# A two-layer encoder kernel on one core: the mixer's front in another order, and 1/rms spread over rows by two products

## The chip, the core and the metric

The kernel runs on one NeuronCore of one Trainium2 chip, as one launch. The metric is the device time of that launch in microseconds. Engines are named as in the profile: PE is TensorE (PEld its weight loads), DVE is VectorE, ACT is ScalarE, POOL is GpSimd, SP is SyncE, which here only issues DMA transfers.

## What is computed

Two sequences, one of 512 rows (s) and one of 1024 rows (p), each 1024 wide in float32, go through the same two layers. The reference, cut:

```python
def rms_norm(x, g):
    return x * rsqrt(mean(x * x, axis=-1, keepdims=True) + 1e-6) * g

def fourier_mixer(x, g, w):                     # layer 0
    h = rms_norm(x, g).reshape(b, s, 8, 128)
    return real(fft2(h, axes=(1, 3), norm="ortho")).reshape(b, s, d) @ w

def attention_mixer(x, ...):                    # layer 1: 8 heads, 2 kv heads, QK norm, rotary
    ...
def swiglu_ffn(x, g, w_gate, w_up, w_down):     # after each mixer, inner width 2816
    h = rms_norm(x, g)
    return (silu(h @ w_gate) * (h @ w_up)) @ w_down

for i in range(2):
    x = x + mixer_i(x)
    x = x + swiglu_ffn(x, ...)
```

## The kernel before, in words

**Precision.** Large products are made of float32 numbers split into a high part (cast to fp32r) and the rest (fp32r as well): `split` makes the high part on ACT and the rest on DVE or POOL, and `mm3` (lines 245 to 249) adds three products, high by high, high by rest, rest by high. Weights are split when they are loaded: `weights` (lines 266 to 279) issues the DMA on SP, casts on ACT (L278) and subtracts on POOL (L279). A few small products use float32 operands directly: a product with `ones` sums columns (L299) or spreads a value (L308).

**Blocks and stages.** The rows lie in three blocks of 512 columns (b = 0 for s, 1 and 2 for p). `weave` runs a main stage, the feed-forward product `ffn` of one block, together with an auxiliary stage for the next blocks, and draws from both generators in proportion to costs in the code. Ahead of this stands the front, in which only s has work: `lead` and `follow` (lines 1172 to 1195). The order on each engine is then made by a scheduler from the order in which the instructions are recorded and from its own estimate of when their operands are there; instructions that go through `pinned` keep their recorded order.

**The front.** The mixer of s has these steps.
1. `load_rows` brings the rows of s in four tiles. `in_rows(gx...)` spreads the gains over all partitions (two calls). `busy(36)` issues 36 float32 products of `ones` with itself.
2. `prepared` (lines 386 to 402): for each of four row tiles a square with a sum on ACT (L393), then four additions or products on DVE (L396 to L399) that fold the rows; then `rsqrt` (lines 282 to 293), twelve steps of 4 columns on DVE (three Newton steps), which gives `r_s`, 1/rms per row.
3. `unit(k, c)`: scales and adds the folded rows (L466 on ACT, L467 on DVE) and splits the result (`comb`). Four units; each needs `r_s`.
4. `along` multiplies the units with the Fourier matrix (`c<-mat_s,comb`); the result is split into `u` (tile `eo`).
5. Beside this `turned_weights` (lines 601 to 655) takes the mixer's weights `wf` through the inner Fourier transform: eight pieces. `operand(n)` adds on DVE (L619) and subtracts on POOL (L620) the two halves of a loaded piece into `f`, casts `f` on ACT (L622) and subtracts on POOL (L623) into `wm`; `product(n)` multiplies (`g<-wm,eo`), splits (`w`), and copies the two results to be written to `cwd` in DRAM, from where p reads them later. The first of the two copies runs on ACT (L644), the second on DVE (L646). The rows for column 64 come as one stacked piece, `raw<-in_wf64`, into `stage`, which `stacked` casts on ACT (L597) and subtracts on DVE (L599).
6. `mixer_projection` multiplies `u` with the turned weights, eight steps n (`c<-eo,w`), adds to the residual, splits, and squares. Then `in_rows(rstd[0])`, and the first feed-forward product `g<-h,w` starts.

**What sets the order between 3 and 5.** `lead` draws one step of `turned_weights` after the steps 1, 3, 6, 8, 10, 12, 14 of the mixer, and records `stacked` after step 4. `follow` draws one more after each of the first four projection steps, and then the rest.

**Spreading.** `in_rows(y)` (lines 302 to 309) is used throughout: for gains, for 1/rms of a block ahead of each `normed` or `moving`, for the keys. For each of four chunks of 128 columns ACT scales the identity by a column of y (L307), and a product with `ones` in float32 (L308) puts that column's values into every partition:

```python
for j in range(4):
    dg = (temp or tmp)(P)
    act.activation(dg, ident, AF.Copy, scale=y[:, j : j + 1])
    pe.matmul(r[:, j * P : (j + 1) * P], ones, dg, start=True, stop=True)
```

Of the kernel before, what the change touches and what calls it, by code (L numbers as in the profile page):

```python
# [10 lines left out]
F32 = mybir.dt.float32  # L11
# [6 lines left out]
P = 128  # L18
# [106 lines left out]
def trunk_kernel(ctx: ExitStack, tc: tile.TileContext, t: dict):  # L125
# [89 lines left out]
    make_identity(nc, ident)  # L215
    ones = cp.tile([P, P], F32, name="ones")
    dve.memset(ones, 1.0)
# [63 lines left out]

    def rsqrt(y, x, scale, scr):

        n = y.shape[-1]
        v, ti, a = (scr[:, k * n : (k + 1) * n] for k in range(3))
        z = col(n)
        dve.tensor_scalar(v, x, scale, EPS, op0=ALU.mult, op1=ALU.add)
        dve.tensor_scalar(ti.bitcast(I32), v.bitcast(I32), 1, None, op0=ALU.logical_shift_right)
        dve.tensor_scalar(z.bitcast(I32), ti.bitcast(I32), -1.0, MAGIC, op0=ALU.mult, op1=ALU.add)
        for k in range(3):  # L290
            dve.tensor_tensor(a, v, z, op=ALU.mult)
            dve.scalar_tensor_tensor(a, a, -0.5, z, op0=ALU.mult, op1=ALU.mult)
            dve.scalar_tensor_tensor(z if k < 2 else y, a, 1.5, z, op0=ALU.add, op1=ALU.mult)

# [7 lines left out]
    def in_rows(y, temp=None, ps=None):  # L302

        r = bank() if ps is None else ps
        for j in range(4):
            dg = (temp or tmp)(P)
            act.activation(dg, ident, AF.Copy, scale=y[:, j : j + 1])  # L307
            pe.matmul(r[:, j * P : (j + 1) * P], ones, dg, start=True, stop=True)  # L308
        return r
# [76 lines left out]
    def prepared(seq, n, ga, gb, sums):  # L386


        s = mpt.tile([P, n], F32, name=f"s_{seq}")
        r = mpt.tile([P, n], F32, name=f"r_{seq}")  # L390
        for c, x in enumerate(whole[seq]):
            sq = raw_tile(D) if seq == "p" else bank2().rearrange("p k n -> p (k n)")
            pinned(act.activation(sq, x, AF.Square, accum_out=s[:, c : c + 1]))  # L393
            y = tl("c", [TB], F32, "cX", pools["psX"])
            f = sums[c]
            dve.tensor_tensor(f[:, 0], ga, x[:, 0:TB], op=ALU.mult)  # L396
            dve.tensor_tensor(y, gb, x[:, TB:D], op=ALU.mult)
            dve.tensor_tensor(f[:, 1], f[:, 0], y, op=ALU.subtract)
            dve.tensor_tensor(f[:, 0], y, f[:, 0], op=ALU.add)  # L399
            yield 4.0  # L400
        rsqrt(r, s, 1.0 / D, bank()[:, 0 : 4 * n])
        return r
# [198 lines left out]
    def turned_weights(w64, dd, odd, alt):  # L601
# [26 lines left out]
        def product(n):  # L628
# [5 lines left out]
            for k in range(2):  # L634
# [7 lines left out]
                c = tl("t", [TB], F32, "tX")  # L642
                if k == 0:
                    act.copy(c, ps)  # L644
                else:
                    dve.tensor_copy(c, ps)  # L646
                sp.dma_start(cwd[h][:, :, k, j, :], c.rearrange("p (n c) -> p n c", n=4))
# [144 lines left out]
    def moving(blocks, gain, ops):  # L792

        tp = open_pool("tT")
        yield 2.0
        r = [in_rows(rstd[b], lambda n: tl("t", [n], F32, "tT", tp)) for b in blocks]
        yield 1.0
# [361 lines left out]
    xrs_s = [slot[:, 6288 + TB * i : 6288 + TB * (i + 1)] for i in range(2)]  # L1159
    stage = tl("raw", [D], F32, "rawF")  # L1160
    slot_a = h_slot("wm", F32R, "B")[:, 0 : 16 * TB].rearrange("p (s h k n) -> p s h k n", s=4, h=2, k=2)
# [10 lines left out]
    def lead():  # L1172
# [3 lines left out]
        for k, v in enumerate(m):  # L1176
            yield v
            if k == 4:
                stacked(w64[0:96], stage[0:96], 64)
            if k in (1, 3, 6) or k in (8, 10, 12, 14):  # L1180
                next(ws)

    def follow():
        m = mixer_projection("s", got_s)
        for k in range(4):
            next(m)
# [176 lines left out]
```

## Time and profile before

| | us |
|---|---|
| median of 3 runs | 3044.05 |
| lowest, highest | 3040.32, 3046.63 |
| the profiled execution | 3041.73 |
| its span, first to last instruction | 3040.0 |
| PE busy in it | 2967.5 |

The profile shows one execution. In a row of a timeline stand the start, the duration, the engine, the line, the operation, and result and operands by the program's names; in brackets how long the engine had been idle before and which instruction ended that. Matmul durations overlap: a 128x512 product shows 0.39 us and starts 0.23 us behind the one before it, so that work on PE is measured from start to start. The granted clock of PE is a share of 2.4 GHz.

### The profile page before, as it was taken

To read this page: it belongs to the slowest core of one execution; us is meant where nothing else is said; L and a number is where in the kernel's file an instruction comes from. 1 tells how busy PE (TensorE), PEld (TensorE's weight loads), DVE (VectorE), ACT (ScalarE), POOL (GpSimd) and SP (SyncE) were. 2 spreads that over 40 slices of the span, in tenths; PEclk is the share of its full clock that TensorE was granted. 3 is DMA by queue.
4 is the path that set the end of the run, shared out by engine and by line. 5 is a ranking of instruction groups with operands and counts; after the bars stand their busy time and mean duration, and the time that the engine had idled before them with its cause. 6 is when DMAs were issued, how large, how long until landed. Compare 5 with 4: busy or idle time off the path is not lost. (4 is left out here: it accounts for less than half of the span.)

```text
span 3040.0 us, 36889 instructions
## 1 busy us (share of the span) xinstructions
PE 2967.5 (98%) x14184; PEld 2435.7 (80%) x14184; DVE 1667.8 (55%) x2883; ACT 1231.3 (41%) x1835; POOL 1282.6 (42%) x652
## 2 busy tenths in 40 slices
PE   7999999999999999999999999999999999999999
PEld 6778888888877788888878788877787787887777
DVE  7785565634556543533474465665236555655566
ACT  5533332423466522333344577776324222222221
POOL 4334444433333644444433311313636644645452
PEclk9999999999999999999999999999999999999999
DMA  6434543332232633433343211212635411111111
GB/s 223 150 111 132 166 139 104 125 104 77 97 98 90 229 131 133 141 106 101 99 142 111 87 59 53 75 51 91 221 121 183 164 56 54 44 56 55 44 55 63
DMA packets 132080, 330.05 MB, mean 109 GB/s; under 512 B 14176, under 2 KB 28512, under 8 KB 131264
## 3 DMA queue, kind: packets, MB, share of 16 engines
q1 hardware_dynamic: 130688, 318.71, 32.3%
q0 software_dynamic: 928, 7.94, 0.7%
q8 instruction: 111, 1.82, 0.3%
q10 hardware_dynamic: 288, 1.05, 0.1%
q14 instruction: 65, 0.53, 0.1%
HBM read 280.45 MB, written 47.19 MB: 108 GB/s over the span
## 5 line engine op out<-in xcount | busy, mean ns | idle before, releaser
L279 POOL TENSOR_TENSOR w<-raw,w 128x1024 fp32r<-128x1024 f32 x354 | 847.2, 2404 | 1308.1 <-ACT w L278 1259.2
L745 DVE TENSOR_TENSOR acc<-c,acc 128x512 f32<-128x512 f32 x704 | 483.0, 689 | 441.4 <-PE c L249 437.3
L278 ACT CAST w<-raw 128x1024 fp32r<-128x1024 f32 x354 | 371.2, 1050 | 562.3 <-PE c L249 270.9
L247 PE MATMUL g<-h,w 128*128 128x512 f32 x1408 | 556.5, 395 | 4.4 <-ACT t L777 4.4
L249 PE MATMUL g<-h,w 128*128 128x512 f32 x1408 | 552.8, 393 | 0.8 <-POOL w L279 0.8
L248 PE MATMUL g<-h,w 128*128 128x512 f32 x1408 | 552.3, 393 | 0.0
L247 PE MATMUL c<-mid,w 128*128 128x512 f32 x1056 | 417.6, 397 | 13.0 <-DVE acc L745 8.8
L248 PE MATMUL c<-mid,w 128*128 128x512 f32 x1056 | 414.2, 392 | 1.8 <-DVE mid L241 1.8
L249 PE MATMUL c<-mid,w 128*128 128x512 f32 x1056 | 413.6, 392 | 0.0
L241 POOL TENSOR_TENSOR w<-raw,w 128x512 fp32r<-128x512 f32 (+1 forms) x178 | 239.6, 1368 | 311.0 <-ACT w L240 290.0
L858 DVE TENSOR_TENSOR acc<-c,acc 128x512 f32<-128x512 f32 x352 | 240.8, 689 | 186.4 <-PE c L249 185.5
L247 PEld LDWEIGHTS g<-h,w 128*128 128x128 f32 x1408 | 265.6, 189 | 57.5 <-ACT t L777 5.4
L249 PEld LDWEIGHTS g<-h,w 128*128 128x128 f32 x1408 | 265.6, 189 | 56.5 <-POOL w L279 1.8
L248 PEld LDWEIGHTS g<-h,w 128*128 128x128 f32 x1408 | 265.7, 189 | 52.0
L247 PEld LDWEIGHTS c<-mid,w 128*128 128x128 f32 x1056 | 198.1, 188 | 75.1 <-DVE acc L745 18.5
L248 PEld LDWEIGHTS c<-mid,w 128*128 128x128 f32 x1056 | 198.9, 188 | 42.0 <-DVE mid L241 3.8
L249 PEld LDWEIGHTS c<-mid,w 128*128 128x128 f32 x1056 | 198.6, 188 | 40.4
L248 PE MATMUL c<-h,w 128*128 128x512 f32 x480 | 188.2, 392 | 3.1 <-POOL h L241 2.9
L247 PE MATMUL c<-h,w 128*128 128x512 f32 x480 | 189.1, 395 | 0.0
L240 ACT CAST w<-raw 128x512 fp32r<-128x512 f32 (+1 forms) x178 | 107.5, 648 | 196.9 <-PE a L249 79.8
L249 PE MATMUL c<-h,w 128*128 128x512 f32 x480 | 187.0, 390 | 0.0
L1073 DVE TENSOR_REDUCE col<-a 128x1 f32<-128x1024 f32 (+1 forms) x96 | 100.4, 1046 | 127.4 <-PE a L249 127.1
(342 smaller groups left out, 4765.5 us busy)
## 6 DMA issues: line engine op xcount, KB each, us to landing
raw<-in_down_dram SPq DMA_DIRECT2D x110, 512.0 KB, 3.5
raw<-in_gate_dram SPq DMA_DIRECT2D x88, 512.0 KB, 3.5
raw<-in_up_dram SPq DMA_DIRECT2D x88, 512.0 KB, 3.6
raw<-in_qkv_dram SPq DMA_DIRECT2D x36, 512.0 KB, 3.9
t<-xres SPq DMA_DIRECT2D x56, 256.0 KB, 3.9
raw<-in_wo_dram SPq DMA_DIRECT2D x24, 512.0 KB, 3.7
raw<-in_gate_dram SPq DMA_DIRECT2D x44, 256.0 KB, 2.6
raw<-in_up_dram SPq DMA_DIRECT2D x44, 256.0 KB, 3.1
```

Of the source, the lines that this page charges most:

```text
L240: act.copy(hi, src)
L241: eng.tensor_tensor(lo, src, hi.bitcast(F32), op=ALU.subtract)
L247: pe.matmul(out, lh, rh, start=first, stop=False)
L248: pe.matmul(out, lh, rl, start=False, stop=False)
L249: pe.matmul(out, ll, rh, start=False, stop=last)
L278: pinned(act.copy(flat[:, 0], raw)) if early else act.copy(flat[:, 0], raw)
L279: pool.tensor_tensor(flat[:, 1], raw, flat[:, 0].bitcast(F32), op=ALU.subtract)
L745: dve.tensor_tensor(acc[dc], ps, acc[dc], op=ALU.add)
L858: dve.tensor_tensor(acc, ps, acc, op=ALU.add)
L1073: dve.tensor_reduce(st[:, 0:1], s_in, op=ALU.max, axis=AX.X)
```

## The change

- `prepared`: for s the four squares are recorded first, one behind the other, the steps of `rsqrt` are pinned, and the mixer yields after every second row tile rather than after each.
- `lead`: a step of `turned_weights` after the steps 0, 1, 2, 4, 6, 8, 10, 12 of the mixer (after 1, 3, 6, 8, 10, 12, 14 before); `stacked` after step 3; `follow` draws one more after three projection steps.
- `stage` takes a buffer of the tag "mid" and not one of the two of "rawF", which `f` uses.
- `product`: both copies for `cwd` run on ACT.
- `in_rows`: the four scaled identities are written side by side, each split into a high part (ACT) and the rest (DVE), and two products of 128x512 with fp32r operands take the place of four of 128x128 in float32. `ones` is made as fp32r and seen as float32 where it was used so.

```diff
-    ones = cp.tile([P, P], F32, name="ones")
+    ones_r = cp.tile([P, P], F32R, name="ones")
+    ones = ones_r.bitcast(F32)
...
-    def rsqrt(y, x, scale, scr):
+    def rsqrt(y, x, scale, scr, keep=lambda ins: ins):
...
         for k in range(3):
-            dve.tensor_tensor(a, v, z, op=ALU.mult)
+            keep(dve.tensor_tensor(a, v, z, op=ALU.mult))
...
     def in_rows(y, temp=None, ps=None):
 
         r = bank() if ps is None else ps
+        dg = [(temp or tmp)(TB, F32R) for _ in range(2)]
         for j in range(4):
-            dg = (temp or tmp)(P)
-            act.activation(dg, ident, AF.Copy, scale=y[:, j : j + 1])
-            pe.matmul(r[:, j * P : (j + 1) * P], ones, dg, start=True, stop=True)
+            js = slice(j * P, (j + 1) * P)
+            split(dg[0][:, js], dg[1][:, js], ident, gain=y[:, j : j + 1])
+        for b in range(2):
+            pe.matmul(r, ones_r, dg[b], start=b == 0, stop=b == 1)
         return r
...
-        for c, x in enumerate(whole[seq]):
+        def square(c, x):
             sq = raw_tile(D) if seq == "p" else bank2().rearrange("p k n -> p (k n)")
             pinned(act.activation(sq, x, AF.Square, accum_out=s[:, c : c + 1]))
+
+        if seq == "s":
+            for c, x in enumerate(whole[seq]):
+                square(c, x)
+        for c, x in enumerate(whole[seq]):
+            if seq == "p":
+                square(c, x)
...
-            yield 4.0
-        rsqrt(r, s, 1.0 / D, bank()[:, 0 : 4 * n])
+            if seq == "p" or c % 2:
+                yield 4.0
+        rsqrt(r, s, 1.0 / D, bank()[:, 0 : 4 * n], *([pinned] if seq == "s" else []))
...
                 c = tl("t", [TB], F32, "tX")
-                if k == 0:
-                    act.copy(c, ps)
-                else:
-                    dve.tensor_copy(c, ps)
+                act.copy(c, ps)
...
-    stage = tl("raw", [D], F32, "rawF")
+    stage = tl("stage", [D], F32, "mid")
...
-            if k == 4:
+            if k == 3:
                 stacked(w64[0:96], stage[0:96], 64)
-            if k in (1, 3, 6) or k in (8, 10, 12, 14):
+            if k < 3 or k % 2 == 0 and k < 14:
                 next(ws)
...
-        for k in range(4):
+        for k in range(3):
             next(m)
             next(ws)
```

DVE, at the end of Newton's steps of s, before the change. `r_s` is 1/rms, `eo` from `raw` the residue of the stacked weights, `f` the addition of a weight piece, `comb` a unit's split result, `w` from `g` a split turned product:

```order
L599 TENSOR_TENSOR eo_150<-raw_152,eo_150 32x1024
L291 TENSOR_TENSOR c_274<-c_274,col_275 128x4
L292 SCALAR_TENSOR_TENSOR c_274<-c_274,col_275 128x4
L293 SCALAR_TENSOR_TENSOR r_s<-c_274,col_275 128x4
L407 TENSOR_TENSOR m_290<-r_s,mask 128x1
L437 TENSOR_SCALAR neg_s<-r_s 128x4
L508 TENSOR_SCALAR t_295<-x_229,r_s 1x512
L408 TENSOR_SCALAR m_290<-m_290 128x1
L241 TENSOR_TENSOR w_328<-g_329,w_328 128x512
L467 SCALAR_TENSOR_TENSOR a_299<-x_229,m_290,a_299 128x512
```

The same place on DVE now:

```order
L292 TENSOR_TENSOR c_274<-c_274,col_275 128x4
L293 SCALAR_TENSOR_TENSOR c_274<-c_274,col_275 128x4
L294 SCALAR_TENSOR_TENSOR r_s<-c_274,col_275 128x4
L630 TENSOR_TENSOR f_288<-raw_255 128x512
L418 TENSOR_TENSOR m_295<-r_s,mask 128x1
L448 TENSOR_SCALAR neg_s<-r_s 128x4
L519 TENSOR_SCALAR t_300<-x_229,r_s 1x512
L419 TENSOR_SCALAR m_295<-m_295 128x1
L478 SCALAR_TENSOR_TENSOR a_304<-x_229,m_295,a_304 128x512
L630 TENSOR_TENSOR f_338<-raw_272 128x512
L242 TENSOR_TENSOR eo_150<-t_300,eo_150 1x512
L242 TENSOR_TENSOR comb_222<-a_304,comb_222 128x512
```

The residue of the stacked weights has left Newton's steps (it stands now behind the first `comb`), and the additions of the third and the fourth weight piece, which stood behind both first units, stand among them.

PE, where the queries' stage of the second block begins, spreading its 1/rms (`c` from `t` and `ones`) among feed-forward products (`g`, `c` from `mid`) and the first products of a projection (`c` from `h`), before the change:

```order
L247 MATMUL c_13807<-mid_13727,w_13351 128x512
L248 MATMUL c_13807<-mid_13727,w_13351 128x512
L249 MATMUL c_13807<-mid_13727,w_13351 128x512
L308 MATMUL c_13140<-t_13141,ones 128x128
L308 MATMUL c_13140<-t_13144,ones 128x128
L308 MATMUL c_13140<-t_13147,ones 128x128
L247 MATMUL c_13176<-h_12514,w_13173 128x512
L308 MATMUL c_13140<-t_13150,ones 128x128
L248 MATMUL c_13176<-h_12514,w_13173 128x512
```

The same place now:

```order
L249 MATMUL g_13745<-h_12199,w_13732 128x512
L311 MATMUL c_13140<-t_13141,ones 128x512
L248 MATMUL c_13176<-h_12514,w_13173 128x512
L311 MATMUL c_13140<-t_13142,ones 128x512
L249 MATMUL c_13176<-h_12514,w_13173 128x512
L250 MATMUL c_13176<-h_12514,w_13173 128x512
```

Four products of 128 columns have become two of 512, with one other product between them.

## Rows read from the trace of the kernel before

**Rows 1.** The page's first part: busy time, share of the span and instructions of each engine.

```profile
PE 2967.5 (98%) x14184; PEld 2435.7 (80%) x14184; DVE 1667.8 (55%) x2883; ACT 1231.3 (41%) x1835; POOL 1282.6 (42%) x652
```

**Rows 2.** Busy time by stretch of the span: stretch in us, its length, busy us of PE, PEld, DVE, ACT and POOL with their instructions, granted clock of PE, share of the DMA engines, GB/s.

```profile
0.00:5.11 5.11, 0.00 (x0) 0.00 (x1) 0.17 (x1) 1.94 (x4) 2.94 (x10) 1.00 0.61 179
...
20.01:57.45 37.44, 26.78 (x110) 19.17 (x109) 32.02 (x59) 22.30 (x43) 22.24 (x14) 0.82 0.65 205
57.45:91.84 34.39, 32.51 (x236) 30.07 (x235) 29.21 (x64) 18.36 (x33) 8.60 (x7) 1.00 0.44 129
91.84:130.00 38.16, 34.87 (x161) 28.54 (x160) 20.93 (x42) 18.75 (x31) 18.00 (x8) 0.96 0.59 207
```

**Rows 3.** PE's waits in the first 130 us: for whom, us in total, times, longest.

```profile
PE c L308 <- ACT t L307: 5.1, 1, 5.1
PE g L247 <- ACT t L644: 4.0, 2, 3.4
PE g L247 <- ACT t L777: 2.5, 1, 2.5
...
```

**Rows 4.** PE's waits from 130 us to the end, the same columns.

```profile
PE a L247 <- ACT p L1077: 12.5, 9, 1.7
...
PE c L308 <- ACT t L307: 1.3, 2, 0.9
...
```

**Rows 5.** DVE in order of time: folding steps, the first of Newton's steps, and so on to the last write into u.

```profile
12.33 1.29 DVE L397 TENSOR_TENSOR c<-c,x 128x512 f32<-128x512 f32 x2
13.53 1.28 DVE L398 TENSOR_TENSOR x<-x,c 128x512 f32<-128x512 f32 x2
...
20.39 0.15 DVE L287 TENSOR_SCALAR c<-s_s 128x4 f32<-128x4 f32 x1
...
24.97 2.54 DVE L599 TENSOR_TENSOR eo<-raw,eo 32x1024 fp32r<-32x1024 f32 x1
...
27.95 0.16 DVE L293 SCALAR_TENSOR_TENSOR r_s<-c,col 128x4 f32<-128x4 f32 x1
...
57.00 0.76 DVE L241 TENSOR_TENSOR eo<-c,eo 128x256 fp32r<-128x256 f32 x2
```

**Rows 6.** DVE's groups of instructions from 20 to 60 us: line, operation, result and operands, shapes, count, busy us, mean ns of one, idle time before them.

```profile
L619 DVE TENSOR_TENSOR f<-raw 128x512 f32<-128x512 f32 x6 | 6.4, 1076 | 1.3 <-DMA raw<-in_wf_dram 1.3
L646 DVE COPY t<-g 128x512 f32<-128x512 f32 x5 | 3.4, 677 | 0.0
...
L467 DVE SCALAR_TENSOR_TENSOR a<-x,r_s,a 128x512 f32<-128x512 f32 x1 | 0.7, 749 | 0.0
...
L496 DVE SCALAR_TENSOR_TENSOR t<-x,r_s,col 128x24 f32<-128x24 f32 x1 | 0.2, 246 | 0.0
```

**Rows 7.** ACT's groups of instructions from 20 to 60 us, columns as in rows 6.

```profile
L644 ACT COPY t<-g 128x512 f32<-128x512 f32 x5 | 2.9, 589 | 0.2
```

**Rows 8.** POOL in order of time, the weight pieces of the front.

```profile
15.06 1.27 POOL L620 TENSOR_TENSOR f<-raw 128x512 f32<-128x512 f32 x1 [11.17 <-DMA raw<-in_wf_dram]
...
24.07 2.35 POOL L623 TENSOR_TENSOR wm<-f,wm 128x1024 fp32r<-128x1024 f32 x1 [2.24 <-ACT wm L622]
26.51 3.35 POOL L620 TENSOR_TENSOR f<-raw 128x512 f32<-128x512 f32 x2
39.69 4.70 POOL L623 TENSOR_TENSOR wm<-f,wm 128x1024 fp32r<-128x1024 f32 x2 [9.83 <-ACT wm L622]
...
63.76 2.40 POOL L623 TENSOR_TENSOR wm<-f,wm 128x1024 fp32r<-128x1024 f32 x1 [1.77 <-ACT wm L622]
```

**Rows 9.** PE in order of time: the projection's first product and the first product of the feed-forward stage.

```profile
57.45 0.39 PE L247 MATMUL c<-eo,w 128*128 128x258 f32 x1
...
91.84 0.39 PE L247 MATMUL g<-h,w 128*128 128x512 f32 x1
```

**Rows 10.** Stretches of 2 us, columns as in rows 2.

```profile
40.00:42.00 2.00, 2.00 (x6) 1.18 (x5) 0.94 (x2) 1.58 (x4) 2.00 (x1) 0.50 0.95 257
50.00:52.00 2.00, 2.00 (x16) 1.85 (x16) 2.00 (x2) 0.92 (x3) 1.92 (x2) 1.00 1.18 341
```

**Rows 11.** Line 308's products over the whole span: count, durations in ns (min/median/max), first and last start.

```profile
L308 PE MATMUL c<-t,ones x136: 270/275/582, 5.1 to 2274.2; 128*128 128x128 f32 x136
...
L308 PE MATMUL a<-t,ones x16: 272/275/349, 105.9 to 115.0; 128*128 128x128 f32 x16
```

**Rows 12.** PE in order of time around the spread for a key.

```profile
738.73 0.39 PE L247 MATMUL g<-h,w 128*128 128x512 f32 x1
738.96 0.64 PE L308 MATMUL c<-t,ones 128*128 128x128 f32 x4
739.36 0.48 PE L247 MATMUL c<-h,w 128*128 128x512 f32 x1
739.68 0.65 PE L308 MATMUL c<-t,ones 128*128 128x128 f32 x4
740.08 0.48 PE L248 MATMUL c<-h,w 128*128 128x512 f32 x1
740.39 0.39 PE L249 MATMUL c<-h,w 128*128 128x512 f32 x1
```

**Rows 13.** Line 307 on ACT: four diagonals in a row in order of time, and one of them over the whole span (ns, min/median/max).

```profile
558.48 1.28 ACT L307 ACTIVATE t<-ident,rs 128x128 f32<-128x128 f32 x4 [4.96 <-DVE rs L293]
...
L307 ACT ACTIVATE t<-ident,rs x36: 384/391/404, 101.7 to 2273.3; 128x128 f32<-128x128 f32 x36
```

More of the change, by code (lines that the diff above doesn't have):

```diff
@@ L286, in rsqrt @@
         z = col(n)
-        dve.tensor_scalar(v, x, scale, EPS, op0=ALU.mult, op1=ALU.add)
-        dve.tensor_scalar(ti.bitcast(I32), v.bitcast(I32), 1, None, op0=ALU.logical_shift_right)
-        dve.tensor_scalar(z.bitcast(I32), ti.bitcast(I32), -1.0, MAGIC, op0=ALU.mult, op1=ALU.add)
+        keep(dve.tensor_scalar(v, x, scale, EPS, op0=ALU.mult, op1=ALU.add))
+        keep(dve.tensor_scalar(ti.bitcast(I32), v.bitcast(I32), 1, None, op0=ALU.logical_shift_right))
+        keep(dve.tensor_scalar(z.bitcast(I32), ti.bitcast(I32), -1.0, MAGIC, op0=ALU.mult, op1=ALU.add))
         for k in range(3):
-            dve.tensor_tensor(a, v, z, op=ALU.mult)
-            dve.scalar_tensor_tensor(a, a, -0.5, z, op0=ALU.mult, op1=ALU.mult)
-            dve.scalar_tensor_tensor(z if k < 2 else y, a, 1.5, z, op0=ALU.add, op1=ALU.mult)
+            keep(dve.tensor_tensor(a, v, z, op=ALU.mult))
+            keep(dve.scalar_tensor_tensor(a, a, -0.5, z, op0=ALU.mult, op1=ALU.mult))
+            keep(dve.scalar_tensor_tensor(z if k < 2 else y, a, 1.5, z, op0=ALU.add, op1=ALU.mult))
     def rstd_cols(y, sq, n):
@@ L795, in moving @@
         yield 2.0
-        r = [in_rows(rstd[b], lambda n: tl("t", [n], F32, "tT", tp)) for b in blocks]
+        r = [in_rows(rstd[b], lambda n, dt: tl("t", [n], dt, "tT", tp)) for b in blocks]
         yield 1.0
```

## The prediction

> **What bounds the kernel now.** I read the page's busy times first: TensorE (PE) is busy for 2967.5 of 3040.0 us, 98%, and no other engine reaches 56% [rows 1]. So only two things can move the time: work that leaves PE, and PE's idle 72.5 us. Second I read the stretches. Of the idle time 21 us lie before 130 us [rows 2]: 5.1 us before the first product, 10.7 us in the stretch from 20.01 to 57.45 us (26.78 busy of 37.44), 1.9 us up to 91.84 us, 3.3 us up to 130 us. The other 51 us are spread over 2910 us. In the stretch 20.01 to 57.45 PE also ran at a mean granted clock of 0.82: at 40 us it stands at 0.50, that is at 1.2 GHz, with gaps in PE's work ahead, and at 50 us it is back at 1.00 [rows 10]. Third come PE's waits. Before 130 us PE waits once for the first diagonals (5.1 us), then above all for copies and an activation of ScalarE (ACT) [rows 3]; after 130 us the largest wait is for attention's exponentials, which the change doesn't touch [rows 4].
>
> Fourth, the front's own chain on VectorE (DVE). It starts Newton's steps at 20.39 us and writes r_s at 27.95 us [rows 5]. Twelve small steps of about 0.2 us are 2.4 us; between them stand a split of a product, an addition and above all the residue of the stacked weights, 2.54 us [rows 5]. Everything of the mixer stands behind r_s. From 20.39 to the last write into u at 57.74 us (57.00 + 0.74) DVE is 37.35 us on its way. The projection's first product starts at 57.45 us and the first gate product at 91.84 us [rows 9]; between the two PE is busy 32.51 of 34.39 us [rows 2].
>
> **The change, part by part.**
>
> *Spreading by two products.* A spread was four fp32 products of 128 columns, two records each, so eight records. There are 152 records [rows 11], so 19 spreads; two stand ahead of the first real work, 17 behind it. What one costs PE is read at 738.96 us: up to 740.39 us there are eight records and two 128x512 products [rows 12]. 1.43 us less two products of 0.23 us (738.73 to 738.96) is 0.97 us. Now it is two products of 128x512 with fp32r operands, of the kind whose pace is 0.23 us: 0.46 us. 17 x (0.97 - 0.46) = **8.7 us less on PE**, which is the bound in all these stages. Bounds: 0, if the new products ran no faster than the old, and 9.
>
> *What the two products wait for.* Before, the first product went as soon as one diagonal was there; four take ACT 1.28 us [rows 13]. Now the first needs all four high parts, some 0.9 us more (1.28 less the 0.39 of one [rows 13]), and the second the last of four new subtractions on DVE. No row shows those at 128x128; between 128x24 (0.246 us) and 128x512 (0.749 us) [rows 6] a straight line gives 0.35 us. 17 x 4 x 0.35 = 24 us of DVE work, hidden beside PE, since DVE is busy 55% [rows 1]; without that cover the normalized operands come later. Both orders put other products between and ahead of the two, so I take 0.2 us of standing per spread, **3.4 us more**; bounds 0 and 0.9 x 17 = 15 us. The value lies near the low end because before the change PE waited for diagonals only twice behind 130 us, 1.3 us together [rows 4]. The Trainium skill (SBUF — State Buffer, "SBUF: two separate sides") says that a DVE instruction with two SBUF inputs and a GpSimd instruction take a shared pair of ports in turn, and whichever starts first holds it to its end. By that rule each subtraction could stand behind a whole POOL instruction, and the sum would be that of the last rival below. The trace agrees where it shows the case: the residue of the stacked weights began inside a POOL piece and ended 1.1 us behind that piece's end [rows 5, 8].
>
> *Front, up to r_s.* The squares now stand in a row on ACT, Newton's steps in a row on DVE, and the stacked weights' residue behind them. Taken away between 20.39 and 27.95 us: the 2.54 us [rows 5]. The order behind VectorE's start also puts the two units of x_140 together, but then an addition waits for the first weights, which POOL also got only at 15.06 us [rows 8], so that nothing is won there. r_s comes at about 25.6 us, 2.5 us earlier; bounds 0 and 3.
>
> *Front, r_s to the last u.* DVE loses the four copies that stand in this stretch (0.68 us each [rows 6], 2.7 us) and gets the residue back. Adding up its new order with 0.6 us for a 128x512 step (four take the 2.4 us from 12.33 to 14.7 [rows 5]), 1.8 for the residue (half-way between its 2.54 us and the 1.1 us that it took once POOL was done) and 1.0 for an addition that meets POOL [rows 6] gives 25.6 us, against 29.6 before (28.11 to 57.74); beside the copies the difference is standing, 1.3 us of it ahead of the additions [rows 6]. ACT gets those copies as well, 0.59 us each [rows 7], and its own list behind r_s also sums to 26 us: it becomes as full as DVE. So neither can end before 51.5 us, and some waits on PE and POOL will stay; I take 54 us, **3.5 us earlier**. The weight pieces don't hold it: POOL stood still from 29.86 to 39.69 us, waiting for a cast [rows 8], and now the additions stand among the units and a second buffer of that tag is free. Its last piece, ended at 66.16 us, should be done by 57.
>
> *Front, projection.* One more of the eight turned products stands ahead of the projection than before, 9 products of 0.23 us, so 2.1 us less remain in a stretch that PE fills; the half clock ahead of it costs what it did. **2 us earlier.** Together the first gate product moves by 5.5 us; bounds 0 and 8.6 (57.74 - 51.2, plus 2.1).
>
> *The first 20 us.* The first spread ends a good microsecond earlier, but behind it the warming products only end earlier too, and PE's next products need the first weight piece, whose halves POOL began to subtract at 15.06 us, when they had landed [rows 8]: nothing.
>
> *SP, POOL.* SP issues as many transfers; the loads of wf are moved ahead of the writes of cwd, whose reader is far off. Nothing.
>
> Sum: -8.7 + 3.4 - 5.5 = -10.8. The profiled execution took 3041.73 us (span 3040.0), so 3030.9, and I forecast **3031 us**. The median of the runs shown, 3044.05, is 2.3 us above the profiled execution; I leave that in the range.
>
> **The rivals.** A measurement of this kernel can tell 0.2%, 6.1 us, from no change.
>
> *Spreads stand still (same or a little faster).* Each of the four subtractions reads two operands in SBUF, as the additions f do, and those took 1.08 us on average [rows 6] where POOL was at work, and the residue 2.54 us: it began at 24.97 us, POOL's piece ended at 26.42 us, and the residue at 27.51 us [rows 5, 8]. POOL is busy 42% [rows 1] with pieces of 2.4 us [rows 8]; a subtraction that meets one waits 1.2 us for its rest, 0.5 us on average, and 17 of them take 8.6 us off, all that the products give. Then the front alone is left: 3041.7 - 5.5 = 3036.
>
> *Front gives nothing.* ACT takes DVE's place there: its eight copies stand in one queue with the casts that PE waits for, and each copy also waits for a buffer that a write to cwd must free. Then only the spreads are left: -8.7 + 3.4, 3036.4.
>
> *The new products bring nothing.* If `ones` as fp32r with these operands went at the old pace of 0.97 us per spread and the front's lead were lost at the first gate units, where PE already waits 2.5 us for the activation [rows 3], it stays at 3041.
>
> *Slower.* The same standing, but worse: the four subtractions of a spread meet POOL's pieces not once but so that a spread comes 1.2 us late each time, with PE queued behind its first product in order and every product behind it. 17 x 1.2 = 20.4, less 8.7 and 5.5: 3041.7 + 6.2 = 3048. It decides from 0.84 us per spread on ((8.7 + 5.5) / 17). For it: no row shows the subtractions, and the additions f beside POOL took on average as much as this asks. Against it: POOL idles more than half of the time, and a spread lost its 1.2 us only if the scheduler left no slack. The Trainium skill's rule on the shared ports, named above, would make this case.
>
> **How the numbers follow.** Both gains as summed: 0.58. Spreads stand still: 0.15. Front gives nothing: 0.14. Nothing comes: 0.05. Slower: 0.08. The first lies nearly whole beyond -6.1 us from the median (0.56 of it), the second and third straddle the bound (0.17 of 0.29): faster 0.73, slower 0.08, same 0.19. Range: from 3022, where the front's 8.6 and the spreads' 9 come with hardly a wait and the execution is like the profiled one, to 3043, which takes in all cases but the slower one.
>
> **What would show it.** Right: two records of 128x512 per spread at a pace of about 0.23 us; r_s written near 25.6 us; the last write into u near 54 us; the first gate product near 86 us; POOL's last piece of wf before 60 us; PE busy some 10 us shorter with about the same idle time. Wrong: waits of PE for L245 or L244 at the spreads of 0.5 us and more each; subtractions at 128x128 of over 1 us beside POOL; u late behind ACT's copies; or idle time of PE grown by as much as its busy time shrank.

## The result: slower, and the profile after

The changed kernel takes 3049.02 us (median of 12 runs, 3043.97 to 3053.47), the kernel before 3042.68 beside it (3038.26 to 3046.63): a ratio of 1.0024 [1.0017, 1.0032]. The forecast was 3031 us. In the profiled execution the span grew by 7.5 us, from 3040.0 to 3047.5. The page's first part of the changed kernel, to be held against [rows 1]:

```profile
PE 2965.1 (97%) x14070; PEld 2430.7 (80%) x14070; DVE 1702.6 (56%) x2951; ACT 1235.3 (41%) x1843; POOL 1283.6 (42%) x652
```

PE's busy time fell by 2.4 us, not by some 10, and its idle time rose by 9.9 us to 82.4. The products themselves did nearly what was forecast. From 404.95 to 1524.91 us before and from 404.10 to 1518.69 us after, PE runs the same products but for those of nine spreads (columns as in [rows 2]). Its work there shrank by 4.42 us, 0.49 per spread, and the stretch by 5.37 us: so far the spreads paid. First before, then the change:

```profile
404.95:1524.91 1119.96, 1110.72 (x5142) 915.16 (x5141) 547.82 (x953) 432.89 (x622) 468.47 (x206) 1.00 0.37 119
```

```profile
404.10:1518.69 1114.59, 1106.30 (x5089) 910.28 (x5087) 558.15 (x982) 431.68 (x621) 468.77 (x206) 1.00 0.36 119
```

What took that and more stands in three places: the front, a spread in `moving` (the stage that scales blocks 1 and 2 by their 1/rms ahead of the last feed-forward products), and the last attention. PE's waits of the change, before 130 us (first fence) and behind (second), answer to [rows 3, 4]:

```profile
PE c L311 <- ACT t L244: 7.5, 2, 6.5
PE c L651 <- POOL wm L634: 4.7, 3, 2.0
PE c L651 <- ACT wm L633: 2.6, 2, 1.6
PE g L248 <- ACT t L785: 1.7, 1, 1.7
...
```

```profile
PE a L248 <- ACT p L1085: 11.1, 8, 1.8
...
PE c L311 <- DVE t L245: 4.6, 2, 3.4
...
PE c L248 <- DVE pt L242: 3.1, 2, 1.8
...
PE a L248 <- ACT t L954: 2.6, 1, 2.6
```

The wait for L245, the subtraction of a spread, is new: 3.4 us of it fall on one spread. The wait for `pt` is new too, and it lies in attention, where nothing was changed.

**The front.** VectorE in order of time, then POOL, then PE, as in [rows 5, 8, 9]:

```profile
21.70 0.15 DVE L288 TENSOR_SCALAR c<-s_s 128x4 f32<-128x4 f32 x1
23.84 0.69 DVE L242 TENSOR_TENSOR w<-g,w 128x512 fp32r<-128x512 f32 x1 [1.99 <-ACT w L241]
24.44 0.16 DVE L289 TENSOR_SCALAR c<-c 128x4 int32<-128x4 int32 x1
...
26.45 0.16 DVE L294 SCALAR_TENSOR_TENSOR r_s<-c,col 128x4 f32<-128x4 f32 x1
...
29.97 2.12 DVE L630 TENSOR_TENSOR f<-raw 128x512 f32<-128x512 f32 x1
32.02 1.76 DVE L242 TENSOR_TENSOR eo<-t,eo 1x512 fp32r<-1x512 f32 x1
...
63.15 0.42 DVE L242 TENSOR_TENSOR eo<-c,eo 128x256 fp32r<-128x256 f32 x1 [1.15 <-ACT eo L241]
```

```profile
18.87 2.36 POOL L634 TENSOR_TENSOR wm<-f,wm 128x1024 fp32r<-128x1024 f32 x1
...
61.00 5.29 POOL L634 TENSOR_TENSOR wm<-f,wm 128x1024 fp32r<-128x1024 f32 x2 [1.80 <-ACT wm L633]
```

```profile
21.04 0.48 PE L248 MATMUL g<-wm,eo 128*128 128x512 f32 x1
...
60.12 0.28 PE L248 MATMUL c<-eo,w 128*128 128x258 f32 x1
...
93.21 0.39 PE L248 MATMUL g<-h,w 128*128 128x512 f32 x1
```

r_s came 1.5 us earlier (26.61 against 28.11), but the last write into u 5.8 us later (63.57), the projection 2.7 us later, the first gate product 1.4 us later. The row to look at is the clock. The 2 us stretches of the change, as in [rows 10]:

```profile
40.00:42.00 2.00, 2.00 (x7) 1.27 (x5) 1.42 (x2) 1.17 (x3) 2.00 (x1) 0.50 0.99 261
48.00:50.00 2.00, 2.00 (x10) 1.68 (x9) 2.00 (x4) 1.45 (x3) 1.37 (x1) 0.57 0.59 234
50.00:52.00 2.00, 2.00 (x14) 1.55 (x13) 0.92 (x2) 0.38 (x1) 0.20 (x1) 1.00 0.74 150
```

In stretches of 0.25 us PE ran at 1.2 GHz from 25.75 to 49.75 us, 24 us; before it did so from 28.0 to 34.75 and from 38.25 to 45.0 us, 13.5 us. PE's idle time (its standing, as it is called below) from 20 to 36 us is 8.1 us in both.

**The spread in `moving`.** PE, VectorE and POOL of the change around 2276 us:

```profile
2276.58 0.40 PE L311 MATMUL c<-t,ones 128*128 128x512 f32 x1
...
2281.03 0.50 PE L311 MATMUL c<-t,ones 128*128 128x512 f32 x1 [3.38 <-DVE t L245]
```

```profile
2275.46 4.40 DVE L245 SCALAR_TENSOR_TENSOR t<-ident,rs,t 128x128 fp32r<-128x128 f32 x2 [0.47 <-ACT t L244]
```

```profile
2274.95 4.76 POOL L280 TENSOR_TENSOR w<-raw,w 128x1024 fp32r<-128x1024 f32 x2 [11.30 <-ACT w L279]
```

Two subtractions began 0.51 us behind the first of two pieces of POOL and took 4.40 us; they ended at 2279.86, the pieces at 2279.71. The median of one subtraction is 0.34 to 0.35 us, as the durations of line 245 show (ns, min/median/max):

```profile
L245 DVE SCALAR_TENSOR_TENSOR t<-ident,rs,t x36: 334/343/2425, 103.7 to 2280.6; 128x128 fp32r<-128x128 f32 x36
...
L245 DVE SCALAR_TENSOR_TENSOR t<-ident,yk,t x24: 339/346/1686, 738.5 to 1682.0; 128x128 fp32r<-128x128 f32 x24
```

Nine of the 76 subtractions took over 1 us, but behind 130 us only two spreads made PE wait. Behind this wait PE ran at 0.57 of its clock for 3.5 us:

```profile
2281.53:2285.00 3.47, 3.47 (x11) 2.71 (x10) 2.91 (x5) 1.24 (x2) 1.80 (x2) 0.57 0.75 221
```

**The last attention.** From TensorE's first scores to the Newton step near 2270 us no changed instruction runs but `moving`'s first spread at the very end, and yet the stretch grew by 7.9 us (before first, then the change):

```profile
1702.80:2272.26 569.46, 550.39 (x2994) 458.17 (x2995) 297.76 (x508) 349.97 (x497) 174.25 (x81) 1.00 0.29 92
```

```profile
1697.52:2274.83 577.31, 554.10 (x2999) 460.63 (x2999) 307.69 (x517) 352.73 (x499) 176.48 (x82) 0.99 0.28 93
```

Some of it is feed-forward work that moved in (676 of its products between the first score and the last value, 671 before); 4.1 us more are standing, 23.2 for 19.1.

### The profile page after: what moved, and what is told of

The parts are those of the page before. It is cut to its first block, busy times and chain, and to the rows that moved or that the text cites. A ratio compares the mean times of both kernels' runs of the same rounds, so it can differ in the third digit from the quotient of the medians.

```text
span 3047.5 us, 36740 instructions
## 1 busy us (share of the span) xinstructions
PE 2965.1 (97%) x14070; PEld 2430.7 (80%) x14070; DVE 1702.6 (56%) x2951; ACT 1235.3 (41%) x1843; POOL 1283.6 (42%) x652
## 4 chain that ended last, share of the span: by engine, by line
PE 81%; DVE 4%; issue 2%; POOL 2%; DMA 2%; ACT 2%; SPq 0%; POOLq 0%; ACTq 0%; DVEq 0%
PE c L248 12%; PE c L249 12%; PE c L250 12%; PE g L250 10%; PE g L248 10%; PE g L249 10%; PE a L248 5%; PE a L250 5%; PE a L249 4%; PE c L1099 2%; DVE col L1082 1%; POOL w L280 1%; PE c L1032 1%; DMA x<-xres 1%; DMA raw<-in_down_dram 1%
```

## Experiments

Four landmarks cut each execution: the first gate product; the Newton step near 1245 us; the one near 2270 us, which closes the last attention and its projection; the end. "Stands" is PE's idle time from the first scores of the last attention (near 1697 us) to the landmark near 2270. "Half clock" is where the granted clock stood at 0.50 between 20 and 60 us. "Order" names the sequence of score, transpose, value and feed-forward products on PE in that attention, read from the programs: B is that of the kernel before, N that of the change, other letters further ones.

| kernel | ratio to before | to gate | to 1245 | to 2270 | to end | stands | order | half clock |
|---|---|---|---|---|---|---|---|---|
| before | 1 | 91.8 | 1153.6 | 1026.9 | 767.7 | 19.1 | B | 28.0-34.75, 38.25-45 |
| e12, the same again | - | 92.1 | 1154.3 | 1026.4 | 768.5 | 18.2 | B | 24.5-34.75, 38-45 |
| change | 1.0024 [1.0017, 1.0032] | 93.2 | 1149.3 | 1032.3 | 772.7 | 23.2 | N | 25.75-49.75 |
| e11, the same again | - | 93.5 | 1147.6 | 1033.1 | 772.4 | 25.4 | N | 26.25-50.25 |
| e1 rows only | 1.0024 [1.0014, 1.0035] | 94.0 | 1153.0 | 1030.9 | 769.3 | 25.0 | N | 26.25-46.75, 50.25-53.5 |
| e2 front only | 0.9977 [0.9967, 0.9987] | 88.5 | 1151.0 | 1027.4 | 765.2 | 18.9 | B | 27.0-40.75 |
| e3 moving old | 0.9989 [0.9981, 0.9998] | 93.3 | 1152.6 | 1032.4 | 764.9 | 24.6 | N | 26.0-50.0 |
| e4 columns | 1.0014 [1.0005, 1.0022] | 88.8 | 1153.9 | 1036.0 | 768.2 | 23.4 | P | 27.75-41.5 |
| e5 late old | 0.9971 [0.9959, 0.9984] | 88.7 | 1147.2 | 1027.0 | 763.4 | 21.6 | Q | 26.5-40.25 |
| e6 warm | 1.0014 [1.0005, 1.0023] | 89.6 | 1148.5 | 1031.6 | 771.6 | 23.3 | N | 31.25-34.75, 38.25-41.5 |
| e7 front, pace 0.70 | 1.0087 [1.0074, 1.0101] | 88.5 | 1150.7 | 1043.3 | 781.6 | 21.8 | R | 26.25-40.0 |
| e8 change, pace 0.70 | 1.0062 [1.0048, 1.0075] | 93.1 | 1152.4 | 1049.0 | 764.2 | 26.7 | S | 25.5-49.5 |
| e9 front, q 0.38 | 0.9989 [0.9979, 0.9998] | 88.6 | 1150.6 | 1027.3 | 769.5 | 18.7 | B | 26.5-40.0 |
| e10 late old, warm | 0.9968 [0.9956, 0.9980] | 91.0 | 1151.1 | 1027.8 | 764.6 | 21.6 | Q | 35.75-42.75 |
| e13 eleven new | 0.9977 [0.9968, 0.9985] | 90.3 | 1153.3 | 1028.0 | 764.2 | 19.2 | B | 21.25-41.75 |
| e14 only the 14th | 0.9982 [0.9973, 0.9991] | 87.9 | 1149.6 | 1024.8 | 765.0 | 20.3 | Q | 25.75-39.25 |
| e15 only the 15th | 0.9982 [0.9973, 0.9991] | 88.8 | 1150.9 | 1028.0 | 765.5 | 19.3 | B | 27.25-40.75 |
| e16 14th to 17th | 1.0006 [0.9996, 1.0016] | 91.0 | 1149.1 | 1034.1 | 765.7 | 23.9 | N | 25.75-46.25 |
| e17 copies back | 1.0005 [0.9996, 1.0014] | 95.9 | 1153.6 | 1028.3 | 765.1 | 19.2 | B | 27.75-58.5 |

The stretches come from one profile each. Kernels with the same instructions up to 1245 us (the change, e3, e11, e8) differ by 5 us in the second stretch, so a difference of 2 or 3 us there says nothing. The gate is not steady either: e2, e7, e9, e14, e15 and e16 run the same instructions in the front, and it came between 87.9 and 91.0 us; the change, e3, e5, e8 and e11 share another front, and it came once at 88.7 and four times from 93.1 to 93.5. Over all kernels with the changed front and without products added, the gate goes with the length of the half clock: 13.5 to 13.75 us with 87.9 to 88.8, 20.5 with 90.3 and 91.0, 24 with 93.1 to 93.5, and in e17, where copies go back to VectorE, 30.75 with 95.9. The two stretches behind 1245 us repeat better, but half clock for some us at a time enters them as well.

**e1 and e2: the two parts alone.** e1 is the kernel before with the new `in_rows`; e2 is the change with the old one:

```
-        dg = [(temp or tmp)(TB, F32R) for _ in range(2)]
         for j in range(4):
-            split(dg[0][:, js], dg[1][:, js], ident, gain=y[:, j : j + 1])
-        for b in range(2):
-            pe.matmul(r, ones_r, dg[b], start=b == 0, stop=b == 1)
+            dg = (temp or tmp)(P)
+            act.activation(dg, ident, AF.Copy, scale=y[:, j : j + 1])
+            pe.matmul(r[:, j * P : (j + 1) * P], ones, dg, start=True, stop=True)
```

> The kernel before with the spreads by two products alone; front, squares, Newton's steps and copies as before. Theory A (the loss is made by the spreads: in moving a subtraction on VectorE stands behind GpSimd's pieces, 6 us, and the scheduler's changed order costs 5.8 us between the last row of qkv and the out projection, against about 5 us that the products save): slower than before by 4 to 8 us. Rival B (the loss is made in the front, by the half clock from 26 to 50 us and what follows): about 4 to 6 us faster than before. Rival C (the order of the woven stages is a lottery which any change of costs draws anew, the spreads themselves cost at most 6 us in moving): between 5 us faster and 5 us slower, with another sum for the stretch of attention than in the changed kernel.

> The changed kernel with the old spreads (four fp32 products of 128 columns and one diagonal each); only the front's order, the pinned Newton steps and the copies on ScalarE are left of the change. Theory A: the first gate product 1 us later than before (near 93), the rest as before: 0 to 2 us slower than before, no wait in moving. Rival B: slower by 5 to 8 us, like the whole change. Rival C: within 5 us of before on either side, by the stretch from 1690 to 2270 us.

The spreads alone make the whole loss, 1.0024; the front alone gains 0.23%. Theory A holds for e1. For e2 it had the sign wrong: in the front without the new spreads the first gate product moves from 91.8 to 88.5 us. Rival B falls. But the two parts do not add up to the change, which would then be level with the kernel before: with the new spreads the front's gain is lost in four executions of five (93.1 to 93.5 us at the gate).

**e3: only `moving`'s two spreads in the old form.** `in_rows(..., old=True)` at that call takes the old body.

> The changed kernel with only the two spreads in moving in the old form (four diagonals on ScalarE, four fp32 products). Theory A and C: the wait of 3.4 us of TensorE for L245 near 2280 us and the half clock behind it go, so 5 to 6 us faster than the changed kernel (about as fast as before, 3041 to 3043). If the wait in moving is not the cause of the 6 us lost there (rival D: moving would have lost them anyway to its loads or to GpSimd's pieces), the same as the changed kernel, 3048.

The ratio fell from 1.0024 to 0.9989, more than the 5 to 6 us expected. The last stretch went from 772.7 to 764.9 us and the wait for L245 there is gone, so the cause in `moving` is shown: rival D falls. The stretches ahead stayed the change's in the profiled execution, which at 3044.95 us was one of the slowest of eleven (3032.97 to 3046.07); where the faster ones gained the rest was not profiled. The wait itself is 3.4 us of the 7.8. In the change 10.5 us at half clock come with it (from 2282, 2333 and 2364 us), in e3 none; e1, with the same wait and 3.5 us at half clock, took 769.3 us there. And the meeting hangs on the order: in e8, with the same new spreads, four subtractions in `moving` met no piece (1.13 us together), and the last stretch took 764.2 us.

**e4: the split on the columns**, 128x4, in place of the diagonals.

```
-            split(dg[0][:, js], dg[1][:, js], ident, gain=y[:, j : j + 1])
+        dve.tensor_copy(hi, y)
+        dve.tensor_tensor(lo, y, hi.bitcast(F32), op=ALU.subtract)
+        for b, v in enumerate((y, lo)):
+            for j in range(4):
+                act.activation(dg[b][:, j * P : (j + 1) * P], ident, AF.Copy, scale=v[:, j : j + 1])
```

> The changed kernel with the split of a spread's diagonals made on the four columns (128x4 on VectorE: one copy, one subtraction) and all eight diagonals of 128x128 on ScalarE: no 128x128 subtraction on VectorE is left. Theory A: no spread can stand for 4.4 us behind GpSimd, so moving gives 5 to 6 us back; ScalarE takes 1.3 us more per spread, which costs under 0.3 us each behind other products: 3040 to 3044, 4 to 8 us faster than the changed kernel. Rival E (ScalarE's eight diagonals stand in its queue and make the spreads as late as the subtractions did): within 2 us of the changed kernel. Rival C: the order behind 1690 us is drawn anew, plus or minus 5 us.

1.0014: 3 us faster than the change by the ratios, less than expected, and the intervals overlap. PE no longer waits for L245 in `moving`; the last stretch is 4.5 us shorter. Rival E's wait, for ScalarE's diagonals behind 130 us, is 1.1 us at one spread, so it does not explain the rest. But the order became P, and 1245 to 2270 us took 1036.0 us, the longest of the kernels with the pace untouched.

**e5 to e8.** e5 uses the old body from the last woven stage on (`late_[0] = True` at the head of `aux_3`); e6 adds products to the front (`warm(w, half, count)` issues `count` times `pe.matmul(o, dd[:, 0], w[:, half, i % 2])` into a bank of its own); e7 and e8 change `paced(attend((1, 2)), 0.65)` to 0.70 in e2 and in the change.

```
             pinned(act.copy(w[:, 0], f))
+            warm(w, 0, {1: 8, 2: 6}.get(n, 0))
             pool.tensor_tensor(w[:, 1], f, w[:, 0].bitcast(F32), op=ALU.subtract)
+            warm(w, 1, {1: 6}.get(n, 0))
```

> The changed kernel with the new spreads up to the end of the second layer's first woven stage and the old ones from the last woven stage on (its qkv's spreads and moving's). Theory C (the 10 to 13 us that all kernels with new spreads lose between 1571 and 2272 us come from the order in which the scheduler weaves attention with the feed-forward, which any change of costs draws anew): this order is a third one, neither that of before nor that of the change; the stretch from the Newton step near 1570 to that near 2272 us takes between 700 and 714 us, and nothing says which; total 3034 to 3046. Theory F (the new spreads themselves, their subtractions on VectorE, slow that stretch): with the old spreads it takes 702 us as in e2, and the total is e2's less some 1 to 2 us for the earlier spreads: 3032 to 3036.

> The changed kernel with 20 products of 128x512 more in the front, whose results nobody reads: 8 and 6 behind the two halves of weight piece 1, 6 behind the first half of piece 2, all where TensorE stood between 23 and 32 us. Theory G (what the front lost is TensorE's half clock from 25.9 to 49.7 us, which follows on TensorE standing from 23 us on): the half clock comes later or ends earlier, the first gate product moves from 93.2 to 88 to 90 us, the whole is 3 to 5 us faster than the changed kernel. Rival H (front bound by VectorE's and ScalarE's chain whatever the clock is): the clock rises and the first gate product stays at 92 to 94 us, total as the changed kernel, 3047 to 3050.

> e2 (front's change, old spreads) with one number changed: attention of blocks 1 and 2 is woven at pace 0.70 in place of 0.65, which draws another order between 1690 and 2270 us (this instruction order differs from that of before, which e2 has exactly). Theory C: the stretch 1571 to 2272 us moves by several us from e2's 701.8, most likely upwards to 706 to 714. Theory F: within 2 us of 702, since no spread is changed.

> The changed kernel with the same one number at 0.70: another order between 1690 and 2270 us, with all spreads new. Theory C: the stretch differs from the changed kernel's 712 us by several us, either way (702 to 716). Theory F: 710 to 714, as in every kernel with new spreads so far.

e5 is 0.9971 (3032.05 us median). Its third order costs nothing over 1245 to 2270 us (1027.0). It does not decide between C and F: the total is theory F's and below C's, while the stretch from 1555.9 to 2262.9 us, 707.0 us, is C's and not F's. e6: with 20 idle products (products whose results nobody reads) the half clock shrank from 24 to 6.75 us and the first gate product moved from 93.2 to 89.6 us, as theory G said and against rival H. The whole time does not confirm it: the gain of 0.10% lies within what the intervals allow, and r_s came later (28.44 us). e7 and e8 show how much an order can be worth: one number, no other instruction, and e2 becomes 1.1% slower, the change 0.4%. Their stretches, 717.7 and 728.7 us, lie outside the ranges of both theories; as a test of C and F they are weak, since the pace itself also moves work from stretch to stretch.

**e9 to e12.** e9 is e2 with `paced(qkv(2, ...), 0.38)`, e10 is e5 with e6's products, e11 and e12 the two kernels again.

> e2 (front's change, old spreads) with one number changed: the last qkv is woven at pace 0.38 in place of 0.40. By it the order of scores, transposes, values and feed-forward products on TensorE in the attention of blocks 1 and 2 becomes exactly the changed kernel's, with no spread of the new form anywhere. Theory C (the loss between 1571 and 2272 us lies in this order): that stretch takes 710 to 714 us as in the changed kernel, with 23 to 26 us of TensorE standing, and the total rises by 3 to 10 us over e2's 3034.8. Theory F (the subtractions of the new spreads slow it): 702 us with 20 us of standing, total as e2's.

> e5 (new spreads up to the last woven stage, old ones in it) with the 20 idle products of e6 in the front. Theory G (whether the half clock in the front ends near 40 or near 50 us differs from execution to execution of the same front, and the idle products take the late end away): 1 to 4 us faster than e5's 3032.1, with the first gate product near 89 us. Rival: the products cost as much as they give, 3031 to 3034.

> The changed kernel a second time, for its front alone. Four kernels with the same instructions up to 550 us (the change, e3, e8, e5) gave the first gate product at 93.2, 93.4, 93.1 and 88.7 us. Theory G (the end of the half clock is drawn anew at each execution): either near 93 with the half clock to 49.7 us or near 89 with its end at 40.3 us. The attention stretch again 712 us, the spread in moving again with a wait of 3.4 us.

> The kernel before a second time, for its front and its stretches: first gate product at 91.8 as in its first profile, if its front is steady; 4 us off if the half clock in it is drawn anew as well. Stretch 1571 to 2272 us: 701 to 702 again.

e9's premise was wrong: its order is B, that of before, not the change's, so it could not decide; it repeated e2's attention (569.7 us, 18.7 of standing), with a last stretch 4 us longer: PE ran at half clock there for 10.5 us (from 2292.75 and from 2320.25 us), where e2 did so only in its last 2 us. e10 is level with e5 (0.9968), as its rival said: the idle products shorten the half clock and delay r_s (28.91 us), and the first gate product stands at 91.0. e11 repeats the change to 0.3 us at the first gate product and has the same waits for `pt` in attention, 3.1 us. So the half clock to about 50 us is the usual case of the changed kernel (also in e3 and e8); but e5, with the same instructions up to 550 us, left it at 40.25. There POOL began its first piece at 14.17 us, against 14.97, and all behind it followed, r_s at 25.03. A lead of about 1 us went with 4.5 us at the gate; that it is the cause is not shown, since e13's r_s came at 26.98 us and its gate product at 90.3. e12 repeats the kernel before: 92.1 us at the gate, attention as it was.

**e13 to e16: which spreads redraw the order.** The new body only for the calls named (`if not (2 < calls[0] < 14)` takes the old one in e13, and so on).

> The changed kernel with only its 3rd to 13th spreads in the new form (the gains' two in the front and the six from 1517 us on in the old). TensorE's order in the last attention is then that of before. Theory C: the stretch from the first scores (1697 us) to the Newton step near 2270 takes 569 to 570 us with 18 to 19.5 us of standing as in before and e2; the total is e2's 3034.8 less 11 x 0.2 to 0.5 us: 3029 to 3033. Theory F: 572 to 578 us there, since most of the new spreads are in, and a total of 3036 to 3042.

> e2 with one spread in the new form, the 14th, at 1517 us. The scheduler's order in the last attention becomes e5's. Theory C: the stretch takes 575 to 576 us with 21 to 22 us of standing as in e5 and e10, though one spread of two products is the only difference from e2. Theory F: 569 to 571 us as in e2, since one spread's four subtractions cannot cost 6 us behind it.

> e2 with one spread in the new form, the 15th, at 1565 us. The order in the last attention stays that of before. Theory C and F alike: 569 to 571 us with 18 to 19.5 us of standing, total within 2 us of e2's 3034.8. It is the control of e14.

> e2 with four spreads in the new form, the 14th to the 17th (1517 to 1683 us). The order in the last attention becomes exactly the changed kernel's. Theory C: 577 to 580 us there with 23 to 25.5 us of standing, as in the changed kernel, and VectorE's pt late for TensorE twice (3.1 us together) as there; total 3036 to 3043. Theory F: between e2 and the change, 570 to 574 us.

This settles it. e16 has four new spreads, all ahead of the last attention, and the change's order; it took 577.0 us there with 23.9 of standing. Its waits on PE in that attention are the change's, the one for `h` apart (3.0 us for 2.1):

```profile
PE a L248 <- ACT p L1094: 10.4, 7, 1.8
PE a L250 <- POOL w L242: 3.8, 2, 2.6
PE c L248 <- DVE pt L242: 3.1, 2, 1.8
PE c L249 <- POOL h L242: 3.0, 4, 1.5
PE c L1108 <- ACT p L1096: 1.8, 2, 1.5
```

e13, with eleven new spreads and order B, took 571.7 us with 19.2 of standing, and neither wait for `pt` nor for L1096 is there. One new spread, the 14th, draws order Q (e14); its neighbour leaves B (e15). Theory C predicted e16; theory F, 570 to 574 us, falls. The other profiles agree, whatever spreads they have: the seven of order B took 569.1 to 571.7 us from the first scores on, with 18.2 to 19.2 of standing, the six of order N 577.0 to 579.7 with 23.2 to 25.4. Three things did not come as C said: e14's stretch took 574.5 us with 20.3 of standing, a little under its range; order Q cost nothing from 1245 us on (1024.8 us; the attention starts earlier and takes in 711 feed-forward products for B's 671); and e13's 571.7 is 1.7 us over its range. And e13 gained nothing over e2: eleven spreads, 0.5 us of PE each, cannot be seen in the time (0.9977 both).

**e17: the copies.** e2 with every second `act.copy(c, ps)` a `dve.tensor_copy` again.

> e2 (front's change, old spreads) with every second copy of the turned weights back on VectorE; the last attention's order is that of before. If the copies are a gain, as the prediction's sum has it (four of 0.68 us off VectorE's chain): first gate product 1 to 3 us later than e2's 88.5, total 3036 to 3038. If ScalarE's queue made them a loss (the rival 'front gives nothing'): first gate product at 85 to 88 and 3032 to 3034. If neither engine's queue sets the front's end: within 1 us of e2 at the first gate product, total 3034 to 3036.

1.0005: e2's whole gain is gone, more than expected, so without the copies' move the front gains nothing; the move alone was not run. (The times lie in two groups, four from 3038.3 to 3039.7 and eight from 3042.0 to 3045.8; the profile is of the second, and the first is still above e2's median of 3034.8.) r_s is that of e2 (25.35 us); the difference stands behind it, in 30.75 us at half clock and a first gate product at 95.9 us. PE was busy there and at half speed:

```profile
56.00:58.00 2.00, 2.00 (x11) 2.00 (x10) 1.41 (x3) 1.83 (x4) 2.00 (x3) 0.50 0.36 140
```

## Why the prediction was wrong, point by point

Against the forecast the change lost 18 us: it took 7.5 us more than the profiled execution before, not 10.8 less. By stretch: to the first gate product +1.4 for -5.5; to 1245 us -4.3 for -2.5 (eight spreads at the forecast's 0.31 us each); to 2270 us +5.5 for -2.2 (seven); to the end +5.0 for -0.6.

- *Spreading by two products, -8.7 us on PE.* Nearly right in size: 0.49 us per spread measured over nine, and 0.31 to 0.61 for a single one. In e1 PE is busy for 2960.2 us, 7.3 less than before, and idle for 14.5 more.
- *What the two products wait for, 3.4 us.* This step failed, and not by its mean. The subtraction at 128x128 was sized right (0.35 forecast, 0.343 to 0.352 measured), and behind 130 us PE waited for it at two spreads only, 4.6 us, where the sum had 0.2 us at each of 17. One of the two met a pair of POOL's pieces and cost, with the half clock and the late operands behind it, 7.8 us (e3 against the change in the last stretch). The meeting that the rivals "spreads stand still" and "slower" described is real, but it needed one spread, not seventeen at 0.5 or 1.2 us. The rule that the forecast took from the Trainium skill (SBUF — State Buffer, "SBUF: two separate sides") is borne out by the rows at 2275 us: the first subtraction takes until the first piece ends, and the second, with 2.43 us the longest of its row, about as long as the second piece.
- *No term for the order.* The sum priced the spreads where they stand. It had none for what their changed costs do to the scheduler's weaving hundreds of us later: 1032.3 us for 1026.9, with PE busy for about as long (1005.7 us for 1005.3). e16 shows that the order does it.
- *The first 20 us, "nothing".* Wrong. The first two spreads ended at 11.00 us in place of 10.19; from their first diagonal on they took 5.5 us in every profile with the old body, 5.8 to 6.6 with the new one, since all high diagonals and the subtractions stand ahead. The warming products behind them ended later, and PE's first real product moved from 20.01 to 21.04 us. POOL took the next piece's halves ahead of the first residue, which ended at 21.23 (20.47 before). A split that waits for these products stands among Newton's steps (1.99 us at 23.84).
- *Front up to r_s, 25.6 us.* 26.61 in the change, for the reason above as far as the rows show; 25.31 in e2, 25.03 in e5, but 26.98 in e13 with the old spreads there.
- *Front from r_s to u and projection, -5.5 us.* Wrong in the change, where the half clock grew from 13.5 to 24 us; in e2 the gate moved by -3.3. The sentence "the half clock ahead of it costs what it did" is the one that failed: the half clock lasted 10.5 us longer, and in the kernels with this front the gate goes with its length. Why it lasts longer in one execution than in another stays open. POOL's last piece ended at 66.29 us, not before 60, and e2's last write into u came at 59.44.
- *The rival "slower", 3048.* The time came out near it, the mechanism only at one spread; the rest of the loss is the half clock and the order.
- *The rival "front gives nothing".* Its reason, ScalarE's queue, is refuted by e17: with every second copy off ScalarE's queue the front gains nothing, with all of them on it 0.23%.
- *Steps of VectorE.* Beside POOL VectorE's steps in the front were slower than the sum had them: the addition at 29.97 us took 2.12 us, for the 1.0 of the sum, and the split behind it 1.76, for 0.6.
- *The range's lower end.* 3041.7 less 8.6 and 9 is 3024, not 3022; and from 57.74 to 54 us are 3.7 us, not 3.5. Neither slip matters for the outcome.

The lowest ratios are those of e5 and e10: the front's change, the new spreads up to the last woven stage and the old ones in it. The intervals of e2 and e13 overlap theirs, so it is not shown that any new spread is worth keeping.

## What to carry to other kernels

Where a scheduler weaves two streams, price an edit also by the order that it leaves behind it: compare the instruction order of every later stage, and try the edit with neighbouring settings, before a gain of 0.3% is believed. A two-operand step on VectorE that stands ahead of PE is to be priced by its worst meeting with GpSimd's pieces, not by its mean: here 4.40 us for two steps of 0.34. In a front with gaps, look at how long PE runs at half clock, and at more than one execution; but a remedy that delays the chain ahead can cost as much as it gives (e6, e10).

## What was not expected of the hardware

With PE's standing between 20 and 36 us at 8.1 us in both kernels, the half clock lasted 13.5 us in one and 24 in the other; with 8.9 us in e17, 30.75. In the change PE was busy by the profile without a gap from 40 us until the clock rose near 49.75, in e17 for 18.84 of the 20 us from 38 to 58, and both ran at 1.2 GHz there. What decides when it rises was not settled.

```profile
40.00:49.75 9.75, 9.75 (x28) 7.21 (x26) 6.56 (x11) 7.55 (x14) 5.98 (x3) 0.50 0.77 236
```
